# First mixer of a hybrid decoder: where state, query and gate rows are loaded from, and when the head norm and the gate transposes run

## The chip, the cores and the metric

The kernel runs on one core of a Trainium2 chip. A core has five engines with a queue of instructions each: TensorE (PE, matrix products and transposes), VectorE (DVE), ScalarE (ACT), GpSimd (POOL) and SyncE (SP). Each engine takes its own instructions in order and waits on semaphores for the others. Transfers are issued by an engine (here SP and GpSimd) and carried out by 16 DMA engines. The metric is the device time of one execution in microseconds, shown as the median of several runs.

## The reference

One inference step of a two-layer decoder. Layer one is an mLSTM mixer, layer two a forgetting-attention mixer, each followed by a SwiGLU FFN. Two request groups go through the same weights: a prompt of 1024 rows behind 16 meta rows, and 8 decode sequences of 8 rows with a saved state (C, n, m) each. The change lies in the first mixer. Per head and per chunk of rows it computes

```
b      = cumsum(lf)                                   # log-forget gates
m_t    = max(b + m, max_s(b_t - b_s + li_s))
s      = (q k^T) * exp(b_t - b_s + li_s - m_t)        # causal
num    = exp(b + m - m_t) * (q C) + s v
den    = exp(b + m - m_t) * (q n) + sum(s)
h      = num / max(|den|, exp(-m_t))
C_new  = w_c C + sum_s w_g k_s v_s^T ;  n_new = w_c n + sum_s w_g k_s
out    = (rmsnorm(h, mh_g) * sigmoid(og)) @ w_out     # per head norm, output gate
```

All products are in 32-bit floating point; the large ones are made of three products of a high and a low part of each operand.

## The kernel before

All 1104 rows (64 decode rows, 16 meta rows, 1024 prompt rows) are cut into nine slices (`TT`): slice 0 has the 80 decode and meta rows, slices 1 to 8 have 128 prompt rows each. Three slices make one group (`GRP`, `TS`), of 336, 384 and 384 columns.

`phase_a` projects the values (`tm_proj`), then queries and keys (`qk_out`), whose results ScalarE copies out of PSUM (`qk_evict`, L722) and GpSimd's queue writes to the DRAM scratch `qkD` (L723). `rec_prep` computes the gates: the rows `stk` hold the exponents and weights of all heads over time. They are transposed in nine pieces into `tm` (L958, L959), with one PSUM buffer `tps` per piece and two buffers in rotation; small products `wps` (L962, L963) follow. The rows e and w go to the scratch `eD` and `wD`.

`recurrence` then runs slice by slice, with the order of PE, VectorE, ScalarE and GpSimd fixed as written; SP's queue is ordered by the scheduler. In between it calls `f(n)`, which issues n pieces of the remaining projections (`rest_out`: tile `mmA`, weights `wraw` loaded on SP, `whi` cast on ScalarE at L327, `wlo` subtracted on VectorE at L328). One piece is three products. So PE has filler work while the recurrence waits.

For slice i, `chunk_load` fetches `eb` (the gate rows, broadcast), `qk` and `wb` (the decay weights, broadcast): from SP's queue for slice 0 and from GpSimd's for the others. `chunk_decay` makes the exponents of `eb` (L1130, then ScalarE at L1132); `chunk_scores` computes the scores `sps`, multiplies them into `eb` (L1148), transposes the keys (`kps`, L1152) and scales queries in place into `wb` (L1156). `chunk_state` makes the state products `cp` (L1185) and adds them to C (L1189); GpSimd scales C for the next slice (L1192). `chunk_out` makes the outputs `nps` and copies `den` (L1209) and the values (L1215) out.

Slice 0 also has the eight decode states. `first_load` fetches state C (eight transfers, L1110) and n (four, L1112), both on SP's queue. `first_queries` writes the scaled queries `wb` to the scratch `qwD` (L1164, GpSimd) and reads them back in another layout into `q2` (L1168, four transfers on SP). `first_sums` transposes n on PE (`n0p`, L1119). In `chunk_out` VectorE copies parts of q2 into `qm` (L1228), which PE multiplies with the saved states (`nps`, L1233).

After every third slice `norm_heads` normalizes the heads of a group: a few small steps on `fA`, then one multiplication for each of the three slices (L1329). In the loop over slices its steps are taken by `next(norm)` at two places, and at the end of the next slice by a loop that takes all that are left.

From slice 6 on, `g` takes the place of `f`: it issues the filler and one `gate` step. A gate step works on one head of one group: a row of the output gate (`ogc`, from the scratch `ogD`, on GpSimd's queue, L787, four buffers), its sigmoid on ScalarE (L788), a transpose of the head (`ghps`, L1351), the product (L1353) and the split into high and low parts (L340, L341). `ahead()` fetches one row; it is called twice behind slice 5, and then inside `gate` until three rows are ready.

Of the kernel before, what the change touches and what calls it, by code (L numbers as in the profile page):

```python
# [7 lines left out]
F32 = mybir.dt.float32  # L8
# [8 lines left out]
P = 128  # L17
# [659 lines left out]
def phase_a(self, vt):  # L677
# [6 lines left out]
    with ExitStack() as c3:  # L684
# [93 lines left out]
        def heads(pp, tag, op, deep):  # L778
            ready, behind = [], []
            todo = [(t, h) for t in (0, 1, 2) for h in left[t]]  # L780

            def ahead():
                if todo:
                    t, h = todo.pop(0)
                    og = op(self.uid("ogc"))
                    og = og[:, : TS[t][1] - TS[t][0]]
                    nc.gpsimd.dma_start(og, ogD[h, :, TS[t][0] : TS[t][1]])  # L787
                    ready.append([og, lambda: nc.scalar.activation(og, og, AF.Sigmoid)])  # L788
                    if deep == 1:
                        ready[-1].pop()()  # L790

            def rest():
                while behind:
                    behind.pop(0)()

            def gate(t):
                if not left[t]:
                    return False
                while todo and len(ready) < 1 + deep:
                    ahead()  # L800
                for x in ready[: deep]:
                    if len(x) > 1:
                        x.pop()()
                part = self.gate_head(t, left[t].pop(0), v, ready.pop(0)[0], pp, tag)
                if deep > 1:
                    rest()
                behind.append(part)
                if deep == 1:
                    rest()
                return True  # L810
            return gate, ahead, rest
# [39 lines left out]
def rec_prep(self, kp, gates, rp, pp):  # L851
# [3 lines left out]
    if True:  # L855
# [45 lines left out]
        if True:  # L901
# [51 lines left out]
                                    in1=e[:, T0 + P - 1 : T : P].unsqueeze(2).broadcast_to([HA, 8, P]), op=ALU.add)  # L953
            nc.scalar.activation(stk[64:72], b, AF.Exp)
            yield
            for i, (t0, t1) in enumerate(TT):
                ps = pp.tile([P, 104], F32, name=self.uid("tps"), tag="r")
                nc.tensor.transpose(ps[: t1 - t0], stk[:, t0:t1], self.ident[:104, :104])  # L958
                nc.vector.tensor_copy(tm[: t1 - t0, i, :], ps[: t1 - t0])  # L959
            ps = pp.tile([P, 2, 4, 8], F32, name="wps", tag="r")  # L960
            for j in range(4):
                nc.tensor.matmul(ps[:, 0, j, :], selP[:, j, :], w[:, T0 + P - 1 : T : P], start=True, stop=True)  # L962
# [7 lines left out]
def recurrence(self, kp, rec, v, qkD, fill, gate):  # L970
# [7 lines left out]
    def f(n):  # L978
        for _ in range(n):
            next(fill, None)  # L980
        done[0] += n
# [7 lines left out]
    with ExitStack() as cr, self.pool("recAp", bufs=2, space=PSUM) as pp, \  # L989
# [24 lines left out]
        with self.pool("rec2") as sets[2], self.pool("rec1", bufs=2) as rp, self.pool("rec3") as sets[0], \  # L1014
# [9 lines left out]
            for i in range(1, NT):  # L1024
                if i == 4:
                    upto(8 * KT)
                N2 = load(i + 2) if i + 2 < NT else None
                if i + 1 < NT:
                    f(4 if i > 1 else 8)
                    some()  # L1030
                    self.chunk_scores(i + 1, N, rp, *args, f)
                some()
                next(norm, None)
                g(3)
                some()
                self.chunk_state(i, R, *args, wcP, g)
                if i == NT - 1:
                    nn = rp.tile([P, 4], F32, name="nn", bufs=1)
                    nc.vector.tensor_copy(nn, C[i % 2][:, :, DV])
                if N2:  # L1040
                    self.chunk_decay(i + 2, N2, tm, cap)
                next(norm, None)
                for _ in squares:
                    pass
                squares = self.chunk_out(i, R, rp, *args, den, ssq, g, exp=N2 and N2["exp"])
                if i % 3 == 2:
                    for _ in squares:
                        pass
                next(squares, None)
                for _ in norm:  # L1050
                    pass
                norm = self.norm_heads(i // 3, v, rp) if i % 3 == 2 else iter(())
                if i == 5:
                    ahead()
                    ahead()
                    upto(24 * KT)
                    g = lambda n: f(n) or gate(0) or gate(1)
                R, N = N, N2
            rest()
            next(norm)  # L1060
# [19 lines left out]
def chunk_load(self, i, rp, pp, kp, C, v, qkD, eD, wD, tm, eb=None):  # L1080
    nc = self.nc
    t0, t1 = TT[i]
    L = t1 - t0
    q = nc.gpsimd if i else nc.sync
    if eb is None:
        eb = rp.tile([P, HA, P], F32, name=f"eb{i}", tag="eb", bufs=2 if i % 3 == 1 or i == 0 else None)
    qw = rp.tile([P, 4, P], F32, name=f"wb{i}", tag="wb")
    kw = rp.tile([P, HA, DK], F32, name=f"kw{i}", tag="kw")
    qk = rp.tile([P, 8, P], F32, name=f"qk{i}", tag="qk")
    q.dma_start(eb[:L, :, :L], eD[:, t0:t1].partition_broadcast(L))  # L1090
    q.dma_start(qk[:, :, :L], qkD[:, :, t0:t1].rearrange("m p t -> p m t"))
    for a in range(2):
        q.dma_start(qw[a * 64 : a * 64 + 64, :, :L], wD[a::2, t0:t1].partition_broadcast(64))
    return dict(qk=qk, eb=eb, qw=qw, kw=kw)


# [1 line left out]
def first_load(self, R, sp):  # L1098
# [10 lines left out]
        for j in range(4):  # L1109
            nc.sync.dma_start(C0[a * 64 : a * 64 + 64, j, :, :DV], I["state_C"][0, 2 * j + a].rearrange("h k v -> k h v"))  # L1110
    for j in range(4):
        nc.sync.dma_start(n0[j * 8 : j * 8 + 8], I["state_n"][0, 2 * j : 2 * j + 2].rearrange("a h k -> h a k"))  # L1112


@_add(Net)
# [43 lines left out]
@_add(Net)  # L1159
def first_queries(self, R, sp):  # L1160

    nc = self.nc
    qd = self.dram.tile([P, 4, NS], F32, name="qwD")
    nc.gpsimd.dma_start(qd, R["qw"][:, :, :NS])  # L1164
    q2 = R["q2"]
    for a in range(2):
        for z in range(2):
            nc.sync.dma_start(q2[a * 64 : a * 64 + 64, :, z, :], qd[z * 64 : z * 64 + 64])  # L1168
    for qm in R["qms"]:
        nc.gpsimd.memset(qm, 0.0)  # L1170


@_add(Net)
# [1514 lines left out]
```

## Time and profile before

| | us |
|---|---|
| median of 3 runs | 2926.47 |
| lowest and highest run | 2926.18, 2928.61 |
| the profiled execution | 2928.52 |
| span of the profile (first to last instruction) | 2926.8 |
| TensorE busy in the span | 2825.8 |
| VectorE, ScalarE, GpSimd busy | 1721.1, 1312.4, 1006.0 |
| mean granted clock of TensorE | 0.990 |

The gate transposes run near 183 us of the span, slice 0 from about 218 to 294 us, the loop over the slices until about 457 us. In the rows of the trace a line starts with the start and the length in microseconds, then engine, line, operation, output and inputs; `x8` is the number of instructions in the row, and brackets hold the idle time of the engine before it and what ended it. Rows of SPq and POOL with DMA_DIRECT2D are issues of transfers, not the transfers. Rows of a table by stretches hold the busy time of PE, PEld (weight loads), DVE, ACT and POOL, the granted clock, the busy share of the DMA engines and GB/s.

### The profile page before, as it was taken

What the parts mean: (1) busy time and instruction counts of PE and PEld (TensorE: products, weight loads), DVE (VectorE), ACT (ScalarE), POOL (GpSimd) and SP (SyncE); (2) the same over time, 40 slices, a digit from 0 to 9 for tenths busy, and PEclk for the clock granted to TensorE, in tenths of its full rate; (3) what the DMA queues carried; (4) which work ended last, traced back from release to release, by engine and by line L of the source; (5) the groups of instructions that cost most, each with busy time, mean ns of one, the idle gap of its engine ahead of it and who ended that gap; (6) DMA issues with size and microseconds to landing.
All of it is one profiled execution on the core that took longest, in us unless ns stands there. A gap on an engine that the chain in (4) does not pass through costs nothing.

```text
span 2926.8 us, 53724 instructions
## 1 busy us (share of the span) xinstructions
PE 2825.8 (97%) x20542; PEld 2700.4 (92%) x20542; DVE 1721.1 (59%) x3422; ACT 1312.4 (45%) x2620; POOL 1006.0 (34%) x1481
## 2 busy tenths in 40 slices
PE   7998999999999999999999899999999999999998
PEld 7997988999999999999999887777899999999998
DVE  5044555887777755552355443777468778775543
ACT  5122454544444434443344454877344444443432
POOL 2021333165656411115352101454306565641110
PEclk9999999999999999999999999999999999999999
DMA  7047655222222275543443675342412222227652
GB/s 223 9 121 166 168 159 158 79 79 76 88 80 79 86 268 194 204 142 126 144 164 125 225 287 213 129 167 86 147 53 83 77 83 82 77 86 254 218 182 100
DMA packets 316843, 401.37 MB, mean 137 GB/s; under 512 B 32510, under 2 KB 239354, under 8 KB 315562
## 3 DMA queue, kind: packets, MB, share of 16 engines
q1 hardware_dynamic: 279618, 278.44, 29.6%
q0 software_dynamic: 33296, 117.20, 12.1%
q8 instruction: 161, 2.64, 0.4%
q10 hardware_dynamic: 3672, 2.31, 0.3%
q14 instruction: 96, 0.79, 0.1%
HBM read 300.78 MB, written 97.10 MB: 136 GB/s over the span
## 4 chain that ended last, share of the span: by engine, by line
PE 74%; DVE 11%; issue 5%; DMA 5%; ACT 4%; POOL 1%; SPq 0%; DVEq 0%; ACTq 0%; POOLq 0%
PE m L1410 23%; PE dps L267 6%; PE dps L266 6%; PE dps L268 6%; PE tmps L268 4%; PE tmps L266 4%; PE tmps L267 4%; PE mmA L266 2%; PE mmA L267 2%; DVE slot L341 2%; PE mmA L268 2%; PE sp L2475 2%; PE op L2562 1%; DVE s L2479 1%; PE bps L266 1%
## 5 line engine op out<-in xcount | busy, mean ns | idle before, releaser
L341 DVE TENSOR_TENSOR slot<-slot,slot 128x1024 fp32r<-128x1024 f32 (+3 forms) x263 | 268.4, 1023 | 128.5 <-ACT slot L340 122.2
L340 ACT CAST slot<-slot 128x1024 fp32r<-128x1024 f32 (+3 forms) x263 | 206.6, 788 | 230.1 <-PE dps L267 90.3
L1410 PE MATMUL m<-x1h,slot 128*128 128x384 f32 x640 | 177.8, 338 | 1.6 <-DVE vA L1385 0.8
L1410 PE MATMUL m<-x0h,slot 128*128 128x336 f32 x640 | 167.2, 316 | 0.0
L1410 PE MATMUL m<-x2h,slot 128*128 128x384 f32 x480 | 136.0, 338 | 0.0
L413 POOL TENSOR_TENSOR ns<-ns,nq 128x384 f32<-128x384 f32 (+1 forms) x60 | 65.1, 1086 | 206.0 <-ACT nq L411 204.7
L1517 POOL DMA_DIRECT2D hr<-hT x60 | 32.6, 543 | 287.7 <-DVE T_2l L341 70.9
L108 POOL TENSOR_TENSOR slot<-Ht 128x256 f32<-128x256 f32 x80 | 76.9, 971 | 149.2 <-DMA Ht<-in_w_gate_up 144.4
L108 POOL TENSOR_TENSOR slot<-vA 128x256 f32<-128x256 f32 x80 | 75.3, 952 | 149.4 <-DMA vA<-in_w_gate_up 76.5
L341 DVE TENSOR_TENSOR slot<-vA,slot 128x256 fp32r<-128x256 f32 (+3 forms) x101 | 85.3, 846 | 61.9 <-ACT slot L340 61.9
L341 DVE TENSOR_TENSOR slot<-Ht,slot 128x256 fp32r<-128x256 f32 (+3 forms) x101 | 85.3, 846 | 61.7 <-ACT slot L340 61.7
L1410 PEld LDWEIGHTS m<-x1h,slot 128*128 128x128 f32 x640 | 117.3, 188 | 2.8 <-DVE Ht L1385 1.3
L1410 PEld LDWEIGHTS m<-x0h,slot 128*128 128x128 f32 x640 | 113.6, 188 | 0.0
L1410 PE MATMUL m<-x1l,slot 128*128 128x384 f32 x320 | 108.0, 337 | 0.0
L1410 PE MATMUL m<-x0l,slot 128*128 128x336 f32 x320 | 101.5, 317 | 0.0
L1410 PE MATMUL m<-T_2h,slot 128*128 128x384 f32 x320 | 97.0, 344 | 3.8 <-ACT Ht L1416 1.1
L2502 ACT ACTIVATE s<-s,nb 128x272 f32<-128x272 f32 (+7 forms) x126 | 98.9, 787 | 0.0
L2537 ACT COPY th<-tp 128x768 f32<-128x768 f32 (+1 forms) x80 | 73.4, 919 | 53.5 <-PE tp L2529 30.5
L1410 PE MATMUL m<-T_4h,slot 128*128 128x384 f32 x320 | 96.6, 343 | 0.0
L108 POOL TENSOR_TENSOR vA<-vA 128x512 f32<-128x512 f32 (+1 forms) x60 | 85.1, 1419 | 28.4 <-DVE wl0l L341 28.4
L108 POOL TENSOR_TENSOR Ht<-Ht 128x512 f32<-128x512 f32 (+1 forms) x60 | 84.9, 1416 | 28.4 <-DVE wl1l L341 28.4
L1929 DVE TENSOR_REDUCE ss<-sqb 128x4 f32<-128x256 f32 (+1 forms) x72 | 30.2, 419 | 108.2 <-ACT sqb L1928 107.8
(819 smaller groups left out, 10355.2 us busy)
## 6 DMA issues: line engine op xcount, KB each, us to landing
slot<-in_w_down SPq DMA_DIRECT2D x88, 512.0 KB, 4.1
wr<-in_w_down SPq DMA_DIRECT2D x42, 512.0 KB, 5.1
wraw<-in_w_in_a SPq DMA_DIRECT2D x40, 512.0 KB, 3.9
vA<-in_w_gate_up SPq DMA_DIRECT2D x40, 512.0 KB, 4.0
Ht<-in_w_gate_up SPq DMA_DIRECT2D x40, 512.0 KB, 3.9
hr<-hT POOLq DMA_DIRECT2D x46, 384.0 KB, 5.0
kp<-in_cache_k SPq DMA_DIRECT2D x32, 512.0 KB, 6.3
vp<-in_cache_v SPq DMA_DIRECT2D x32, 512.0 KB, 5.6
```

The costliest lines, as they stand in the source:

```text
L108: self.net.nc.gpsimd.tensor_tensor(out=o, in0=a, in1=b, op=op)
L266: mm(ps, sh, mh, start=first, stop=False)
L267: mm(ps, sh, ml, start=False, stop=False)
L268: mm(ps, sl, mh, start=False, stop=last)
L340: self.nc.scalar.copy(hi, src)
L341: self.nc.vector.tensor_tensor(out=lo, in0=src, in1=hi.bitcast(F32), op=ALU.subtract)
L413: (nc.vector if x >= late else nc.gpsimd).tensor_tensor(out=s, in0=s, in1=sq, op=ALU.add)
L1410: nc.tensor.matmul(u.b[b][:, :n], w[p][:, k], x[q][:, k], start=new and k == i == 0, stop=k == 1 and i == 2, skip_group_check=True)
L1517: nc.gpsimd.dma_start(hraw[j], hT[t][:, 2 * c : 2 * c + 2])
L2475: nc.tensor.matmul(ps[z][:, :n], a[r, qs], b[r, at : at + n], start=(y == 0), stop=(y == 2))
L2502: nc.scalar.activation(ss[z, u], ss[z, u], AF.Exp, bias=nb[:, z : z + 1], accum_out=sm[:, u, z : z + 1])
L2537: nc.scalar.copy(th.rearrange("p x z (u h q) -> p h (x z u) q", h=2, q=64)[:, :, :n], pt[:, :, :n])
```

## The change

Four things change, all in the first mixer.

*State and query loads.* For slice 0, `eb` and `wb` are loaded from GpSimd's queue and only `qk` from SP's; the four loads of n and the four loads of q2 move from SP's queue to GpSimd's, the latter behind the two fills of `qm`.

Before, on SP, between the weight loads `wraw` of the filler:

```order
L324 DMA wraw_2659<-in_w_in_a 128x8x128
L1090 DMA eb_2585<-eD 80x8x80
L1091 DMA qk_2588<-qkD 128x8x80
L1093 DMA wb_2586<-wD 64x4x80 x2
L1110 DMA C_2602<-in_state_C 64x8x128 x8
L1112 DMA n_2603<-in_state_n 8x2x64 x4
L1168 DMA q_2594<-qwD 64x4x64 x4
L324 DMA wraw_2720<-in_w_in_a 128x8x128
```

After, on SP:

```order
L324 DMA wraw_2647<-in_w_in_a 128x8x128
L1096 DMA qk_2576<-qkD 128x8x80
L1113 DMA C_2590<-in_state_C 64x8x128 x8
L324 DMA wraw_2708<-in_w_in_a 128x8x128
L324 DMA wraw_2765<-in_w_in_a 128x8x128
```

SP goes from the state C straight to the weights. On GpSimd, after the change, between the writes of `qkD` (before, the same stretch held only those writes, the write of `qwD` and the two fills):

```order
L723 DMA qkD<-stg_2509 128x336
L1090 DMA eb_2573<-eD 80x8x80
L723 DMA qkD<-stg_2537 128x384
L1094 DMA wb_2574<-wD 64x4x80 x2
L1115 DMA n_2591<-in_state_n 8x2x64 x4
L723 DMA qkD<-stg_2644 128x384
L1167 DMA qwD<-wb_2574 512x1x64
L1170 MEMSET qm_2583 128x400
L1170 MEMSET qm_2584 128x400
L1173 DMA q_2582<-qwD 64x4x64 x4
L723 DMA qkD<-stg_2705 128x384
L1195 TENSOR_TENSOR C_2561<-C_2559,wcP 128x516
```

The eleven moved issues stand ahead of the scaling of C, and q2 stands ahead of one more write of `qkD`.

*Gate rows.* `ahead()` now fetches until three rows are ready (two where `heads` is used in the FFN's first part), is called once behind slice 5, and then at the start of every `g`, ahead of the filler. On GpSimd before, at the loads of slice 8:

```order
L787 DMA ogc_4169<-ogD 128x336
L787 DMA ogc_4171<-ogD 128x336
L749 DMA ogD<-stg_4185 128x384
L1090 DMA eb_4188<-eD 128x8x128
L1091 DMA qk_4191<-qkD 128x8x128
L1093 DMA wb_4189<-wD 64x4x128 x2
L749 DMA ogD<-stg_4253 128x384
L787 DMA ogc_4265<-ogD 128x336
L1192 TENSOR_TENSOR C_2573<-C_2571,wcP 128x516
```

and after:

```order
L787 DMA ogc_4157<-ogD 128x336
L787 DMA ogc_4159<-ogD 128x336
L787 DMA ogc_4161<-ogD 128x336
L749 DMA ogD<-stg_4175 128x384
L1090 DMA eb_4178<-eD 128x8x128
L1094 DMA qk_4181<-qkD 128x8x128
L1094 DMA wb_4179<-wD 64x4x128 x2
L749 DMA ogD<-stg_4243 128x384
L1195 TENSOR_TENSOR C_2561<-C_2559,wcP 128x516
```

The third row goes ahead of two writes of `ogD` and four loads.

*Norm.* The loop that took all remaining steps of `norm_heads` takes one. So in the slice after a group only the first multiplication is done at its end, and the second and third come in the next slice: behind the scaled queries (L1156) and behind `chunk_decay`. This holds for the first two groups.

*Gate transposes.* The nine pieces share three PSUM buffers (slice 0, slices 1 to 4, slices 5 to 8), with one copy by VectorE for each. The diff:

```diff
             def ahead():
-                if todo:
+                while todo and len(ready) < 1 + deep:
                     t, h = todo.pop(0)
                     og = op(self.uid("ogc"))
                     og = og[:, : TS[t][1] - TS[t][0]]
                     nc.gpsimd.dma_start(og, ogD[h, :, TS[t][0] : TS[t][1]])
-                    ready.append([og, lambda: nc.scalar.activation(og, og, AF.Sigmoid)])
+                    ready.append([og, lambda og=og: nc.scalar.activation(og, og, AF.Sigmoid)])
...
-                while todo and len(ready) < 1 + deep:
-                    ahead()
+                ahead()
...
-            for i, (t0, t1) in enumerate(TT):
-                ps = pp.tile([P, 104], F32, name=self.uid("tps"), tag="r")
-                nc.tensor.transpose(ps[: t1 - t0], stk[:, t0:t1], self.ident[:104, :104])
-                nc.vector.tensor_copy(tm[: t1 - t0, i, :], ps[: t1 - t0])
+            for i0, i1 in ((0, 1), (1, 5), (5, NT)):
+                ps = pp.tile([P, 4, 104], F32, name=self.uid("tps"), tag="r")
+                L = TT[i0][1] - TT[i0][0]
+                for i in range(i0, i1):
+                    nc.tensor.transpose(ps[:L, i - i0, :], stk[:, TT[i][0] : TT[i][1]], self.ident[:104, :104])
+                nc.vector.tensor_copy(tm[:L, i0:i1, :], ps[:L, : i1 - i0])
...
-                for _ in norm:
-                    pass
-                norm = self.norm_heads(i // 3, v, rp) if i % 3 == 2 else iter(())
+                next(norm, None)
+                if i % 3 == 2:
+                    norm = self.norm_heads(i // 3, v, rp)
                 if i == 5:
                     ahead()
-                    ahead()
                     upto(24 * KT)
-                    g = lambda n: f(n) or gate(0) or gate(1)
+                    g = lambda n: ahead() or f(n) or gate(0) or gate(1)
...
-    q = nc.gpsimd if i else nc.sync
+    q = nc.gpsimd
...
-    q.dma_start(qk[:, :, :L], qkD[:, :, t0:t1].rearrange("m p t -> p m t"))
-    for a in range(2):
-        q.dma_start(qw[a * 64 : a * 64 + 64, :, :L], wD[a::2, t0:t1].partition_broadcast(64))
+    loads = [(qk[:, :, :L], qkD[:, :, t0:t1].rearrange("m p t -> p m t"))]
+    loads += [(qw[a * 64 : a * 64 + 64, :, :L], wD[a::2, t0:t1].partition_broadcast(64)) for a in range(2)]
+    for o, src in loads if i else loads[1:]:
+        q.dma_start(o, src)
+    if i == 0:
+        nc.sync.dma_start(*loads[0])
...
-        nc.sync.dma_start(n0[j * 8 : j * 8 + 8], I["state_n"][0, 2 * j : 2 * j + 2].rearrange("a h k -> h a k"))
+        nc.gpsimd.dma_start(n0[j * 8 : j * 8 + 8], I["state_n"][0, 2 * j : 2 * j + 2].rearrange("a h k -> h a k"))
...
+    for qm in R["qms"]:
+        nc.gpsimd.memset(qm, 0.0)
     for a in range(2):
         for z in range(2):
-            nc.sync.dma_start(q2[a * 64 : a * 64 + 64, :, z, :], qd[z * 64 : z * 64 + 64])
-    for qm in R["qms"]:
-        nc.gpsimd.memset(qm, 0.0)
+            nc.gpsimd.dma_start(q2[a * 64 : a * 64 + 64, :, z, :], qd[z * 64 : z * 64 + 64])
```

## The prediction

> **What bounds the kernel now.** I read the page first, then the busy time by stretches, then the waits of TensorE inside the first mixer, then the rows around each wait.
>
> ```profile
> span 2926.8 us, 53724 instructions
> ...
> PE 2825.8 (97%) x20542; PEld 2700.4 (92%) x20542; DVE 1721.1 (59%) x3422; ACT 1312.4 (45%) x2620; POOL 1006.0 (34%) x1481
> ```
>
> ```profile
> 150.00:480.00 330.00, 306.71 (x2041) 281.31 (x2040) 169.01 (x380) 133.43 (x334) 86.66 (x135) 0.96 0.60 160
> 480.00:2926.80 2446.80, 2386.26 (x17448) 2289.31 (x17447) 1509.87 (x2982) 1124.40 (x2171) 902.19 (x1289) 0.99 0.40 135
> ```
>
> TensorE (PE) is the bound: busy 97% of the span. The change touches only the stretch 150 to 480 us (columns: length, then busy time of PE, weight loads, VectorE, ScalarE, GpSimd; then the granted clock). There PE is idle for 330.0 - 306.7 = 23.3 us, and its clock is 0.96, worth another 330 x 0.04 = 13 us. So at most 36 us, 1.2% of the span, lie in this stretch. What is won there should reach the end, because behind it PE is busy 97.5% of the time (2386.3 of 2446.8).
>
> ```profile
> PE n0p L1119 <- DMA n<-in_state_n: 6.2, 1, 6.2
> PE kps L1152 <- DVE eb L1148: 3.1, 2, 2.4
> PE mmA L266 <- ACT stg L748: 2.9, 2, 2.4
> ...
> PE tps L958 <- DVE tmA L959: 0.8, 4, 0.3
> ```
>
> These are the waits of PE in that stretch that the change aims at (total, times, longest): one of 6.2 us for the state vector n, two for VectorE before the scores, one of 2.4 us for ScalarE's eviction, four short ones in the gate transposes. Together 13 us.
>
> ```profile
> 182.00:186.00 4.00, 3.17 (x18) 2.22 (x17) 1.77 (x9) 0.75 (x2) 0.54 (x1) 1.00 1.01 309
> 186.00:194.00 8.00, 8.00 (x31) 7.81 (x32) 1.67 (x4) 0.75 (x1) 0.00 (x0) 0.57 0.28 79
> ...
> 236.00:246.00 10.00, 9.23 (x44) 8.83 (x45) 1.89 (x3) 2.75 (x5) 1.07 (x1) 0.57 0.52 131
> ...
> 404.00:410.00 6.00, 4.77 (x26) 4.43 (x27) 2.58 (x7) 2.97 (x7) 1.75 (x4) 0.72 0.58 178
> ...
> 418.00:422.00 4.00, 3.84 (x16) 3.63 (x16) 2.00 (x4) 1.66 (x10) 0.00 (x0) 0.58 0.47 135
> ...
> 458.00:462.00 4.00, 2.09 (x12) 1.82 (x13) 1.23 (x1) 2.06 (x3) 1.09 (x2) 1.00 0.64 208
> ```
>
> Behind the waits stands a second loss: the granted clock (third number from the end) falls. The price of each dip is its length times the missing clock: 8 x 0.43 = 3.4 us at 186, 10 x 0.43 = 4.3 at 236, 6 x 0.28 = 1.7 at 404, 4 x 0.42 = 1.7 at 418. Each follows a thin stretch of PE. But the last row shows a stretch in which PE was busy 2.09 of 4 us and kept clock 1.00, so a dip isn't certain behind a gap of that size.
>
> [...]
>
> **Gate transposes.** Nine copies become three, and PE no longer stops for a free bank after every second transpose: 0.8 us of waits go. The matrix product behind them (wps) now needs the bank of the middle group, a copy four times as long as before; below one of the old waits, 0.3 us. I take 0.6 (bounds 0.3 to 0.8). The thin stretch that ends in the dip at 186 gets shorter by that but keeps its small products, so of the 3.4 us I book half, 1.7 (bounds 0 to 3.4).
>
> **State and query loads.** Here is today's order: two pieces of the chain that ended last (the second is one product of PE at full clock), then rows of PE, SP's queue, GpSimd, ScalarE and VectorE, each with start and length:
>
> ```profile
> 229.68 6.85 DMA n<-in_state_n
> ```
>
> ```profile
> 199.44 0.17 PE mmA L266
> ```
>
> ```profile
> 236.77 0.28 PE L1119 MATMUL n0p<-ident,n 32*128 32x32 f32 x1 [6.20 <-DMA n<-in_state_n]
> 236.98 1.98 PE L1185 MATMUL cp<-vA,kw 16*64 16x129 f32 x16
> ...
> 246.81 1.08 PE L1233 MATMUL nps<-C,qm 128*80 128x129 f32 x8
> ```
>
> ```profile
> 220.14 7.13 SPq L1110 DMA_DIRECT2D C<-in_state_C  x8
> 227.32 3.81 SPq L1112 DMA_DIRECT2D n<-in_state_n  x4
> 236.34 2.51 SPq L1168 DMA_DIRECT2D q<-qwD  x4
> 238.95 34.03 SPq L324 DMA_DIRECT2D wraw<-in_w_in_a  x7
> ```
>
> ```profile
> 229.38 0.74 POOL L1164 DMA_DIRECT2D qwD<-wb  x1 [4.49 <-DVE wb L1156]
> ```
>
> ```profile
> 243.25 1.04 ACT L327 CAST whi<-wraw 128x1024 fp32r<-128x1024 f32 x1 [13.67 <-DMA wraw<-in_w_in_a]
> ```
>
> ```profile
> 244.33 1.22 DVE L328 TENSOR_TENSOR wlo<-wraw,whi 128x1024 fp32r<-128x1024 f32 x1 [7.02 <-ACT whi L327]
> 245.47 1.24 DVE L1228 COPY qm<-q 64x32 f32<-64x32 f32 x2
> ```
>
> n is issued behind eight state loads on the same queue and lands at 236.5. On GpSimd's queue it is issued before 225, ahead of the wait for wb, so PE does not stop at n0p. But the next need is the query copy q2: qwD is written at 229.4, SP waits for it until 236.3, and that wait is only hidden by the wait for n. Without it PE goes on from 230.5: n0p and cp (1.4 us at full clock), 24 products at 0.17 us (4.1), and it stands before nps at about 236.9. So what is late next is q2. It can't be issued before 236.3 (nothing makes qwD earlier), and four issues last 2.5 us as on SP, since GpSimd issues such transfers in 0.54 to 0.74 us.
>
> ```profile
> DMA to landing us min/median/max: 2.3/2.3/2.3
> ```
>
> ```profile
> DMA to landing us min/median/max: 3.8/7.1/7.6
> ```
>
> ```profile
> DMA to landing us min/median/max: 10.2/10.2/10.2
> ```
>
> From issue to landing these are q (from SP, its queue empty), wb (lowest from SP, the others from GpSimd beside big loads) and C. Bounds for q2 from GpSimd are 2.3 and 7.6 us; one weight load will still be under way on SP's queue, which is free of q2's wait now and so issues the weights at about 226 instead of 239. I take 3.5: landing at 238.2 + 3.5 = 241.7, qm copied by 242.2, nps at 242.5. VectorE's other step ahead of qm, wlo, gives the same time: weights issued behind C, whose last load lands at about 225 + 10.2 = 235, then 4.3 us for the weights as now (238.95 to 243.25), 1.0 and 1.2 us for the two casts: 241.7. So nps starts 4.3 us earlier than 246.8, and PE waits some 5.6 us at a new place. A clock dip will follow it. Today's dip is over before nps; the new one falls on work behind it. Price between the small dips (1.7) and today's (4.3): 3.0. Net 4.3 - 3.0 = 1.3 us, bounds -4.1 (q2 at 7.6: 4.1 us later, so nps at 246.6 and a full dip) and 10.5 (no wait and no dip: 6.2 + 4.3).
>
> The other moved issues: eb, wb and n of the first slice go between the evictions on GpSimd, by their order in the new program. eb, issued behind the eviction at about 216.5,
>
> ```profile
> L1130 DVE SCALAR_TENSOR_TENSOR eb<-eb,tmA,cap x8: 288/290/296, 205.8 to 207.3; 80x80 f32<-80x80 f32 x8
> ```
>
> ```profile
> 225.35 0.88 DVE L1148 TENSOR_TENSOR eb<-sps,eb 80x320 f32<-80x320 f32 x2 [16.66 <-PE sps L1146]
> ```
>
> at wb's highest price of 7.6 lands at 224; its eight decays (0.29 each, 2.3) and an exponent of no more than a cast's 1.0 would end at 227.4, and VectorE's product with the scores, which starts at 225.4 today, would be 2.0 us late; at the lowest, 3.8, it lands at 220.3 and nothing is late. I take nothing, and 2.0 is in the range. GpSimd stands at q2 until 236.3; queued behind it are one eviction, whose buffer is needed three tiles on, and the first state product, which waits for ScalarE until 244.9 today. Both cost nothing unless q2 is issued after that.
>
> **Gate rows.** The third gate row was issued behind an eviction; now it goes with the first two, twelve microseconds earlier.
>
> ```profile
> 395.24 0.55 POOL L787 DMA_DIRECT2D ogc<-ogD  x1
> ...
> 399.54 0.58 POOL L787 DMA_DIRECT2D ogc<-ogD  x1
> ```
>
> ```profile
> 401.92 0.48 ACT L788 ACTIVATE ogc<-ogc 128x336 f32<-128x336 f32 x1 [1.48 <-DMA ogc<-ogD]
> ...
> 404.69 0.49 ACT L748 COPY stg<-mmA 128x384 f32<-128x384 f32 x1
> ```
>
> ScalarE waited 1.48 us for that row; three table loads around it stay. The eviction at 404.7, for which PE waits 2.4 us, comes at most 1.5 us earlier; the fourth row, issued at 399.5, needs about as long and lands just in time, so I take 0.9 (bounds 0 to 1.5). With the gap at 1.5 us I let the dip at 404 go: 1.7 (bounds 0, 1.7). The later rows move past one eviction at a time, but wait for a buffer that is freed no earlier; nothing.
>
> **Norm dealt out.** The same six multiplications; two of each three move to later places on VectorE.
>
> ```profile
> 352.04 3.50 DVE L1329 TENSOR_TENSOR vA<-vA,fA 80x1024 f32<-80x1024 f32 x3
> ...
> 412.88 3.50 DVE L1329 TENSOR_TENSOR vA<-vA,fA 128x1024 f32<-128x1024 f32 x3
> ...
> 417.43 1.28 DVE L1148 TENSOR_TENSOR eb<-sps,eb 128x512 f32<-128x512 f32 x2
> ```
>
> ```profile
> 414.69 1.04 ACT L327 CAST whi<-wraw 128x1024 fp32r<-128x1024 f32 x1
> ```
>
> Each block shrinks from 3.5 to 1.2 us. At 357 PE waited 0.7 us (3.1 - 2.4), all of it goes. At 418 VectorE's next step is wlo, and that needs ScalarE's cast, which ends at 415.7; so it can begin only 0.6 us earlier than now. I take 0.7 + 0.6 = 1.3 (bounds 0.7 and 3.1). The dip at 418 stays. The moved pieces stand ahead of state sums and den copies where VectorE idles 1 to 2 us before them; nothing.
>
> **Sum.** 0.6 + 1.3 + 0.9 + 1.3 = 4.1 us of waits, and 1.7 + 1.7 = 3.4 of clock: 7.5. The profiled execution took 2928.5 us (span 2926.8, 1.7 around it), at the upper end of the three runs (2926.2 to 2928.6, median 2926.5). From the median: 2919.0 us.
>
> **Rivals.**
> - The clock is not won (for: a gap of 1.9 us at 458 without dip, so dips follow something else than wait length; against: each dip here stands behind a thin stretch): 2926.5 - 4.1 = 2922.4. [...]
> - The wait for n turns whole into a wait for q2, nps no earlier (for: qwD's 6.9 us is untouched). The term 1.3 becomes -3.0: 7.5 - 4.3 = 3.2, 2923.3.
> - Slower: GpSimd's transfers get little of the engines while C and two weight loads stand on SP's queue, each taking C's 10.2 us: wb, issued at 222, lands at 232, qwD at 243.5, q2 (issued until 245.4) at 255.6, and nps starts at 256.2, 9.4 us later than now, with today's dip of 4.3 behind it. 1.3 becomes -13.7, the sum 7.5 - 15.0 = -7.5: 2934.0. It is a loss from q2 landing at about 248, and one over the bound below from about 254. Against: wb took 7.1 us beside such loads, qwD 6.9 beside C. [...]
> - Better: q2 comes early and no dip follows, all the waits go: 0.6 + 3.4 + 10.5 + 0.9 + 1.7 + 1.3 = 18.4, 2908.1.
>
> **Chances.** A measurement of this kernel tells a change from none at about 0.2%, 5.9 us: faster is below 2920.6, slower above 2932.3. Forecast 0.41, clock not won 0.24, whole wait for q2 0.14, slower 0.11, better 0.10. Faster is the forecast, the better case and a fourth of the second: 0.57; slower is the fourth, 0.11; the rest, 0.32, is within. The range goes from near the better case to the upper side of the q2 case with eb's 2.0 us late: 2909 to 2927.
>
> **What would show it.** PE's wait at n0p is gone and stands at nps for qm, near 242, for 4 to 7 us, the clock half behind it; no wait at tps; the wait for the eviction near 400 under 1.7 us with clock 1.00; the wait before kps near 415 shorter by half a microsecond. Wrong would be: PE still stopping at n0p (wb's and n's landing), a stop at kps near 227 (eb late), or the stretch behind 480 longer than 2446.8.

## The result and the profile after

The changed kernel takes 2912.7 us (median of 5 runs, 2908.4 to 2914.3). The kernel before, run beside it on the same chip, takes 2926.5 us (5 runs, 2924.7 to 2928.6). The ratio is 0.9951, with a 95% interval of 0.9937 to 0.9966: 13.7 us faster. The forecast was 2919.0, 7.5 us faster. The profiled execution of the changed kernel took 2914.3 us, 1.6 above the median.

The page of the changed kernel, its first lines:

```profile
span 2912.4 us, 53731 instructions
...
PE 2819.3 (97%) x20542; PEld 2696.0 (93%) x20542; DVE 1717.8 (59%) x3416; ACT 1312.6 (45%) x2620; POOL 1009.4 (35%) x1492
```

Busy time by stretches, changed kernel (columns as before: length, PE, PEld, DVE, ACT, POOL, granted clock, DMA share, GB/s):

```profile
150.00:480.00 330.00, 314.43 (x2130) 291.48 (x2131) 175.50 (x385) 136.45 (x342) 99.33 (x155) 0.98 0.63 167
480.00:2912.40 2432.40, 2370.90 (x17353) 2273.66 (x17351) 1499.61 (x2970) 1119.74 (x2162) 892.97 (x1280) 0.99 0.41 135
```

In the stretch of the change PE now idles 15.6 us instead of 23.3, and the clock is 0.98 instead of 0.96. The waits of PE there, changed kernel (total, times, longest):

```profile
PE nps L1236 <- POOL C L1195: 3.3, 1, 3.3
PE mmA L266 <- ACT stg L748: 3.2, 2, 2.0
PE n0p L1122 <- DMA n<-in_state_n: 1.6, 1, 1.6
...
PE wps L963 <- DVE tmA L960: 0.2, 1, 0.2
```

The 6.2 us at n0p have become 1.6 there and 3.3 at nps. The stops at tps and at kps are gone. One of the two stops for ScalarE's eviction has shrunk to 1.25 us; the other, of 2.0 us, is new in size (0.6 before). Now the granted clock (third number from the end) at the places of the old dips, and of a new one at 422:

```profile
186.00:190.00 4.00, 4.00 (x16) 4.00 (x15) 0.83 (x1) 0.00 (x0) 0.00 (x0) 0.57 0.46 130
190.00:194.00 4.00, 4.00 (x27) 4.00 (x26) 0.87 (x1) 2.33 (x3) 0.54 (x1) 1.00 0.13 45
...
236.00:242.00 6.00, 4.67 (x24) 4.63 (x25) 1.64 (x7) 1.15 (x2) 4.64 (x6) 0.72 0.93 216
...
396.00:402.00 6.00, 6.00 (x46) 5.44 (x44) 3.16 (x9) 4.21 (x9) 1.39 (x3) 1.00 0.61 178
402.00:406.00 4.00, 3.92 (x34) 3.48 (x34) 3.85 (x6) 3.98 (x12) 1.07 (x2) 1.00 0.37 90
...
422.00:426.00 4.00, 4.00 (x27) 3.35 (x26) 1.09 (x2) 3.10 (x9) 0.54 (x1) 0.60 0.63 181
```

The dip at 186 lasts 4 us instead of 8; the one at 236 costs 6 x 0.28 = 1.7 us instead of 4.3; those at 404 and 418 are gone; the one at 422 (4 x 0.40 = 1.6 us) stands behind the stop of 2.0 us.

That stop is the old one of 404 at a later place: in ScalarE's order the eviction stands behind the sigmoid of a gate row, and the sigmoid waited 2.41 us for the row. ScalarE, changed kernel:

```profile
418.03 0.53 ACT L788 ACTIVATE ogc<-ogc 128x384 f32<-128x384 f32 x1 [2.41 <-DMA ogc<-ogD]
...
420.09 0.50 ACT L748 COPY stg<-mmA 128x384 f32<-128x384 f32 x1
```

To see where the 13.7 us lie, I take the start of the same PE instruction in both traces. The column of differences grows where time is won. 1.6 us are there before anything that the change touches, and belong to no stage.

| same instruction of PE | start before | start after | difference | won in this stage |
|---|---|---|---|---|
| csps, ahead of the change | 150.06 | 148.46 | 1.60 | |
| first wps, behind the gate transposes | 185.89 | 182.81 | 3.08 | 1.5 |
| first sps of slice 0 | 224.44 | 219.99 | 4.45 | 1.4 |
| n0p | 236.77 | 227.72 | 9.05 | |
| first nps with qm | 246.81 | 237.34 | 9.47 | 5.0 |
| first nps of the third head | 251.58 | 243.63 | 7.95 | -1.5 |
| kps of slice 4 | 357.33 | 348.50 | 8.83 | 0.9 |
| ghps near 411 | 410.94 | 399.49 | 11.45 | 2.6 |
| kps near 418 | 418.16 | 404.44 | 13.72 | 2.3 |
| cp behind it | 422.18 | 406.89 | 15.29 | 1.6 |
| last row of the mixer compared | 498.95 | 483.55 | 15.40 | 0.1 |

From 1.60 to 15.40 are 13.8 us, about as much as the medians differ (13.7). From the last row to the end of the span both kernels take about the same (2427.9 and 2428.8 us).

### The profile page after: what moved, and what is told of

Read it like the earlier page. It is cut to its first block, busy times and chain, and to the rows that moved or that the text cites. A ratio compares the mean times of both kernels' runs of the same rounds, so it can differ in the third digit from the quotient of the medians.

```text
span 2912.4 us, 53731 instructions
## 1 busy us (share of the span) xinstructions
PE 2819.3 (97%) x20542; PEld 2696.0 (93%) x20542; DVE 1717.8 (59%) x3416; ACT 1312.6 (45%) x2620; POOL 1009.4 (35%) x1492
## 4 chain that ended last, share of the span: by engine, by line
PE 74%; DVE 11%; DMA 5%; issue 5%; ACT 4%; POOL 1%; ACTq 0%; DVEq 0%; POOLq 0%; SPq 0%
PE m L1413 23%; PE dps L267 6%; PE dps L266 6%; PE dps L268 6%; PE tmps L266 4%; PE tmps L268 4%; PE tmps L267 4%; PE mmA L266 2%; DVE slot L341 2%; PE mmA L267 2%; PE mmA L268 2%; PE sp L2478 1%; PE op L2565 1%; DVE s L2482 1%; PE bps L266 1%
```

## The experiments

In the expectations, A is the reading of the table above (each part wins what its stage shows) and B the rival that the text names. Each profiled execution was compared with the one of the kernel before in the same way. Stages, in us won:

| kernel | transposes 150-224 | loads 224-252 | norm, 252-357 | gate rows 357-411 | norm, 411-422 | 422-499 |
|---|---|---|---|---|---|---|
| changed | 2.9 | 3.5 | 0.9 | 2.6 | 3.8 | 0.1 |
| after_again | 2.8 | 3.5 | 0.7 | 2.6 | 3.3 | 1.1 |
| only_tps | 2.9 | -0.2 | -0.3 | 1.9 | 0.0 | 0.0 |
| only_loads | 0.1 | 4.9 | -0.1 | 0.0 | 1.6 | -0.7 |
| only_gate | -0.1 | 0.2 | 0.0 | 2.6 | 0.1 | 0.5 |
| only_norm | 1.4 | 0.3 | 0.9 | 0.4 | 3.8 | -1.5 |
| no_norm | 1.4 | 3.6 | -0.3 | 2.6 | -0.6 | 1.6 |
| no_tps | 1.4 | 5.1 | 0.7 | 2.6 | 3.8 | 0.3 |
| q2_sp | 1.4 | -2.3 | 0.5 | 2.6 | 3.8 | -2.7 |
| c_first | -12.2 | 7.2 | 0.7 | 2.6 | 3.8 | -1.1 |
| direct_q2 | 2.9 | 2.2 | 0.9 | 2.6 | 3.6 | 0.7 |

Each row is one execution: that of only_loads took 2915.3 us where its kernel's median is 2922.2, that of q2_sp 2926.9 where the median is 2920.9. Two cells show a gain in a kernel that lacks the part for that stage: 1.9 in only_tps (357-411) and 1.6 in only_loads (411-422). There PE stopped (1.98 us at 401.8 and 2.35 us at 410.9), but the clock stayed at 1.00 behind the stop. PE and the stretch behind it, only_loads:

```profile
410.88 0.66 PE L1155 MATMUL kps<-ident,qk 128*128 128x128 f32 x4 [2.35 <-DVE eb L1151]
```

```profile
411.00:415.00 4.00, 4.00 (x36) 3.62 (x37) 3.28 (x8) 1.39 (x9) 0.00 (x0) 1.00 0.50 135
```

So a dip can also stay away by itself. Of the four kernels without the gate rows three have the dip behind that eviction, and of the five without the norm's part four have the one behind kps; the eight with the gate rows and the seven with the norm's part have none there.

**Each part alone.** Four kernels, each the one before with one part of the change.

only_loads:

```diff
-    q = nc.gpsimd if i else nc.sync
+    q = nc.gpsimd
...
+    for o, src in loads if i else loads[1:]:
+        q.dma_start(o, src)
+    if i == 0:
+        nc.sync.dma_start(*loads[0])
...
-        nc.sync.dma_start(n0[j * 8 : j * 8 + 8], I["state_n"][0, 2 * j : 2 * j + 2].rearrange("a h k -> h a k"))
+        nc.gpsimd.dma_start(n0[j * 8 : j * 8 + 8], I["state_n"][0, 2 * j : 2 * j + 2].rearrange("a h k -> h a k"))
...
-            nc.sync.dma_start(q2[a * 64 : a * 64 + 64, :, z, :], qd[z * 64 : z * 64 + 64])
...
+            nc.gpsimd.dma_start(q2[a * 64 : a * 64 + 64, :, z, :], qd[z * 64 : z * 64 + 64])
...
```

> Only the state and query loads are moved. Theory A (each part works by itself, and the offsets between the two traces tell its worth): 3.5 us faster than before, 2923.0; TensorE stops less than 2 us at n0p and 3 to 4 us at nps for the query copy, the clock dip behind it costs under 2 us. Theory B (the loads only bring the wait from one place to another, the offset was won by what the transposes shifted ahead): within 1.5 us of before, nps starts no more than 2 us earlier.

only_gate:

```diff
-                if todo:
+                while todo and len(ready) < 1 + deep:
...
-                while todo and len(ready) < 1 + deep:
-                    ahead()
+                ahead()
...
-                    ahead()
                     upto(24 * KT)
-                    g = lambda n: f(n) or gate(0) or gate(1)
+                    g = lambda n: ahead() or f(n) or gate(0) or gate(1)
```

> Only the gate rows are fetched ahead. Theory A: 2.6 us faster than before, 2923.9; the wait for the eviction near 404 falls from 2.4 to about 1.3 us and the clock stays at 1.00 there; the wait of 2.4 us at kps behind it stays. Theory B (the waits from 400 to 420 hang together: a shorter first wait also shortens the one at kps): 4 us or more.

only_norm:

```diff
-                for _ in norm:
-                    pass
-                norm = self.norm_heads(i // 3, v, rp) if i % 3 == 2 else iter(())
+                next(norm, None)
+                if i % 3 == 2:
+                    norm = self.norm_heads(i // 3, v, rp)
```

> Only the norm is dealt out. Theory A: the wait at kps near 418 goes whole, since the weights' low part on VectorE needs a cast that is long done: 2.3 us and its clock dip 1.6, and 0.9 at 357: 4.8 us faster, 2921.7. Theory B (the prediction's: VectorE's low part waits for ScalarE's cast of that moment, and only with the gate rows ahead does the wait go): 1.3 us, and TensorE still stops about 1.8 us at kps.

only_tps:

```diff
-            for i, (t0, t1) in enumerate(TT):
-                ps = pp.tile([P, 104], F32, name=self.uid("tps"), tag="r")
...
+            for i0, i1 in ((0, 1), (1, 5), (5, NT)):
+                ps = pp.tile([P, 4, 104], F32, name=self.uid("tps"), tag="r")
...
```

> Only the gate transposes are put in three groups. Theory A: 2.9 us faster, 2923.6; the products behind the transposes run 1.5 us earlier, and the stretch of half clock is one of about 3.4 us instead of two. Theory B (the length of the dip has nothing to do with the waits and differs from run to run): 0.6 to 1.5 us, and a dip of 7 us as before.

Against 2926.0 us (33 runs) they took, in 11 runs each: only_loads 2922.2, ratio 0.9988 [0.9979, 0.9997]; only_gate 2923.0, 0.9988 [0.9979, 0.9997]; only_norm 2922.7, 0.9988 [0.9979, 0.9997]; only_tps 2926.7, 1.0001 [0.9992, 1.001]. So three parts win 3 to 4 us each, and the transposes nothing that this measurement shows. The four medians add up to 9.4 us, 4.3 less than the whole; the intervals, 2.6 us to either side for each part, don't exclude 13.7. The times alone don't tell A from B here; the rows do, for three of the parts.

In only_loads nps comes 5.1 us earlier in its stage, which excludes B; PE stops there for 1.6 us, not for 3 to 4. In only_tps neither reading fits whole: wps comes 1.5 us earlier and the dip is short, as A says, and yet no time is won. only_gate, waits of PE between 398 and 404: the stop for the eviction is 1.3 us, as in the changed kernel, where it was 2.4 before. The stop of 2.35 us at kps stays (414.5), so B is out.

```profile
PE mmA L266 <- ACT stg L748: 1.3, 1, 1.3
```

only_norm, PE's kps near 412 without any wait, and the clock behind it:

```profile
412.49 0.66 PE L1152 MATMUL kps<-ident,qk 128*128 128x128 f32 x4
```

```profile
414.00:418.00 4.00, 4.00 (x37) 3.59 (x36) 4.00 (x7) 2.29 (x12) 0.68 (x1) 1.00 0.45 131
```

The norm's part alone removes the stop of 2.4 us there, and with the stop the dip is gone, together 3.8 us. A's mechanism holds; its 4.8 us don't show in the median, which is 3.3 lower.

**The whole without one part.** no_norm is the changed kernel with the old loop over `norm`:

```diff
-                next(norm, None)
-                if i % 3 == 2:
-                    norm = self.norm_heads(i // 3, v, rp)
+                for _ in norm:
+                    pass
+                norm = self.norm_heads(i // 3, v, rp) if i % 3 == 2 else iter(())
```

> The changed kernel without the norm dealt out: three multiplications in one block again. Theory A: 4.8 us slower than the changed kernel (the waits at 357 and at kps come back, with the clock dip behind kps), 2917.5. Theory B (the prediction's size): 1.3 us slower, 2914.0.

no_norm took 2918.0 us (10 runs), ratio 0.9972 [0.9963, 0.9982]: 9.4 us faster than the kernel before, where the whole is 12.6 (after_again, below) to 13.7 faster. That is 3.2 to 4.3 us for the norm, nearer to A than to B; but the intervals overlap, and it is the rows that show the part. PE's kps near 409 stops again and the clock falls behind it:

```profile
409.09 1.11 PE L1155 MATMUL kps<-ident,qk 128*128 128x128 f32 x4 [2.88 <-DVE eb L1151]
```

```profile
410.00:414.00 4.00, 4.00 (x29) 3.77 (x28) 2.06 (x4) 0.99 (x8) 0.00 (x0) 0.68 0.43 124
```

Behind these stages, from 422 to 499, only_norm shows -1.5 and no_norm 1.6 against 0.1: the norm may give back about 1.5 us of its 4.7 there. That column runs from -2.7 to 1.6, so this is not shown.

no_tps is the changed kernel with the old nine pieces, and after_again the changed kernel itself, beside it on the same chip:

```diff
-            for i0, i1 in ((0, 1), (1, 5), (5, NT)):
-                ps = pp.tile([P, 4, 104], F32, name=self.uid("tps"), tag="r")
...
+            for i, (t0, t1) in enumerate(TT):
+                ps = pp.tile([P, 104], F32, name=self.uid("tps"), tag="r")
...
```

> The changed kernel with the nine gate transposes as before. Theory A (the transposes are worth 2.9 us, as the offsets of the traces say, and the part alone only missed it by the scatter of the later stages): 2 to 3.5 us slower than the changed kernel of this call, and a dip of 7 us at 185 again. Theory B (the part alone told it: nothing): within 1 us.

> The changed kernel once more, beside the two others of this call, for a closer value than its first five runs: 13.7 us faster than before if those were typical; 9 to 11 us if the sum of the four parts alone (3.9 + 3.0 + 3.3 - 0.7 = 9.5) is its worth.

no_tps took 2917.6 us (6 runs), ratio 0.9969 [0.9957, 0.9982]; after_again 2914.4 (5 runs, 2908.9 to 2917.8), ratio 0.9959 [0.9946, 0.9973]. By these medians the transposes are worth 3.2 us, by only_tps less than nothing. The traces settle what is regular in it. In all seven kernels with three groups wps comes 1.5 us earlier, in none of the others. The dip behind it is another matter. The stretch 184 to 194 of no_tps (old pieces) and of no_norm (new groups):

```profile
184.00:194.00 10.00, 9.63 (x46) 8.95 (x47) 2.67 (x9) 1.04 (x1) 0.24 (x1) 0.83 0.44 129
```

```profile
184.00:194.00 10.00, 10.00 (x43) 9.95 (x44) 1.59 (x4) 1.63 (x3) 0.54 (x1) 0.67 0.21 60
```

A long dip leaves 0.66 or 0.67 (3.3 to 3.4 us lost), a short one 0.83 (1.7 lost). Short: four of the seven with the new groups, two of the five with the old pieces. So the 1.4 us of clock that the changed kernel won there aren't shown to come from the change. What the part is worth in time stays open, since the intervals of these runs overlap; 1.5 us are regular in the traces.

**Who holds q2.** In the changed kernel, PE reaches nps near 234 and stands until 237.3. Rows of PE, GpSimd, SP's queue, ScalarE and VectorE, changed kernel:

```profile
227.72 0.22 PE L1122 MATMUL n0p<-ident,n 32*128 32x32 f32 x1 [1.60 <-DMA n<-in_state_n]
...
237.34 1.87 PE L1236 MATMUL nps<-C,qm 128*80 128x129 f32 x8 [3.26 <-POOL C L1195]
```

```profile
224.93 0.75 POOL L1167 DMA_DIRECT2D qwD<-wb  x1 [4.36 <-DVE wb L1159]
...
232.80 2.47 POOL L1173 DMA_DIRECT2D q<-qwD  x4 [6.31 <-DMA qwD<-wb]
...
235.84 1.15 POOL L1195 TENSOR_TENSOR C<-C,wcP 128x516 f32<-128x516 f32 x1
```

```profile
214.94 9.07 SPq L1113 DMA_DIRECT2D C<-in_state_C  x8
```

```profile
233.78 1.05 ACT L327 CAST whi<-wraw 128x1024 fp32r<-128x1024 f32 x1 [8.65 <-DMA wraw<-in_w_in_a]
```

```profile
234.86 1.22 DVE L328 TENSOR_TENSOR wlo<-wraw,whi 128x1024 fp32r<-128x1024 f32 x1 [6.66 <-ACT whi L327]
236.48 0.76 DVE L1231 COPY qm<-q 64x32 f32<-64x32 f32 x2 [0.40 <-DMA q<-qwD]
```

The view names the scaling of C as the releaser, but VectorE's copy of q2 into qm ends later (237.2 against 237.0). That copy waited only 0.4 us for q2, because VectorE was at wlo until 236.1: q2 and the weights arrive almost together. From the write of qwD to the first issue of q2 pass 7.9 us.

q2_sp puts the four loads of q2 back on SP's queue; the rest is the changed kernel.

```diff
-            nc.gpsimd.dma_start(q2[a * 64 : a * 64 + 64, :, z, :], qd[z * 64 : z * 64 + 64])
+            nc.sync.dma_start(q2[a * 64 : a * 64 + 64, :, z, :], qd[z * 64 : z * 64 + 64])
```

> The changed kernel, but the four query copies q2 stay on SP's queue, ahead of the weights. Theory A (the queue of q2 counts because the weights stand behind it: the weights are issued at 235, their cast and low part end at about 241.5, and the query copies on VectorE stand behind those): nps starts about 4 to 5 us later than in the changed kernel, and it is 3 to 5 us slower, 2916.5. Theory B (only the landing of the scratch qwD counts, whichever queue reads it back): within 1 us of the changed kernel, 2912.7.

It took 2920.9 us (11 runs) against 2927.4 (26 runs), ratio 0.9981 [0.9972, 0.999]. Waits of PE and rows of SP's queue and ScalarE, q2_sp:

```profile
PE nps L1236 <- POOL C L1195: 7.9, 1, 7.9
```

```profile
233.72 2.50 SPq L1173 DMA_DIRECT2D q<-qwD  x4
236.32 20.45 SPq L324 DMA_DIRECT2D wraw<-in_w_in_a  x5
```

```profile
240.62 1.04 ACT L327 CAST whi<-wraw 128x1024 fp32r<-128x1024 f32 x1 [13.40 <-DMA wraw<-in_w_in_a]
```

SP stands at q2 until 233.7, and the cast of the weights behind it comes 6.8 us later than in the changed kernel (2.1 of which this execution was behind already at the scores). In the trace that turns a gain of 3.5 us in this stage into a loss of 2.3. VectorE's wlo, and the copy into qm behind it, wait for that cast. So A holds. q2_sp is 6.4 us faster than the kernel before, where the whole is 12.6 to 13.7; by these medians the price is 6 to 7 us, and the intervals leave A's 3 to 5 open. What the move of q2 does is to let the weights go; with n, eb and wb moved alone this trace wins nothing. Whether the move of q2 would win anything without that of n was not run.

c_first asks why qwD takes 7.9 us. State C is put ahead of all other loads in the program, to have landed before qwD is written:

```diff
+            R0 = {}
+            self.first_load(R0, sp)
             R = self.chunk_load(0, r0, *args)
...
-            self.first_load(R, sp)
+            R.update(R0)
+            for j in range(4):
+                nc.gpsimd.dma_start(R["n0"][j * 8 : j * 8 + 8], I["state_n"][0, 2 * j : 2 * j + 2].rearrange("a h k -> h a k"))
...
```

> The changed kernel, but the eight loads of the state C are issued on SP ahead of the first slice's qk, so that they don't run beside wb, n and qwD. Theory A (qwD takes 7.8 us because the state's 2 MB stand in the DMA engines): C is issued at about 200 and lands by 213, n lands before TensorE needs it, qwD lands in 4 us or less, q2 by 233, and TensorE does not stop at n0p and at most 1 us at nps: 1.6 + 3.3 us of waits and 1.7 of clock go, 6 us faster than the changed kernel, 2906.5. Theory B (qwD's time is that of 512 small pieces on GpSimd's queue, beside whatever): qwD takes 6 us or more, nps waits as now, only the 1.6 us at n0p go: 2911.

It took 2924.1 us (11 runs), ratio 0.999 [0.9981, 0.9999]. C could not go earlier, since its place is in use until PE is done with what stood there, and qk stood behind it. Waits of SP's queue, then rows of PE and GpSimd, c_first:

```profile
SPq L1117 <- PE mmA L268: 18.8, 1, 18.8
```

```profile
235.66 1.36 PE L1151 MATMUL sps<-qk 64*80 64x80 f32 x16 [13.53 <-DMA qk<-qkD]
```

```profile
242.34 0.75 POOL L1169 DMA_DIRECT2D qwD<-wb  x1 [19.80 <-DVE wb L1161]
...
245.02 2.47 POOL L1175 DMA_DIRECT2D q<-qwD  x4 [1.12 <-DMA qwD<-wb]
```

As a version it fails, but it answers the question: written when C has landed, qwD takes 2.7 us instead of 7.9, against B. C's eight loads, issued there from 217.0 to 226.5, take 8.9 to 10.9 us to land, so they are in by about 237, five us ahead of the write. In the changed kernel they are issued until 224.0 and take 10.3 to 10.5 us, and the DMA share from 225 to 233 is 1.18. So in these two traces its time goes with the load of C beside it.

direct_q2 tries to win what is left: q2 is read straight from `qkD`, without qwD, its decay weights come from `wD` as a second tile (in the place of `km`), and VectorE multiplies the two; the first copy into qm stands ahead of the filler.

```diff
+            nc.gpsimd.dma_start(R["q2"][a * 64 : a * 64 + 64, :, z, :],
+                                qkD[:4, z * 64 : z * 64 + 64, :NS].rearrange("m p t -> p m t"))
+    nc.gpsimd.dma_start(R["w2"].rearrange("p j z t -> p (j z) t"), wD[:, :NS].partition_broadcast(P))
...
+    nc.vector.tensor_tensor(out=R["q2"], in0=R["q2"], in1=R["w2"], op=ALU.mult)
...
```

> The changed kernel, but q2 is read from the scratch of the queries itself with its decay weights beside it, and multiplied on VectorE, so that the scaled queries no longer go out to DRAM and back; the first query copy stands ahead of the weights' low part on VectorE. Theory A (the round trip of qwD is what TensorE waits for at nps): the 3.3 us at nps and its clock dip of 1.7 go, 5 us faster than the changed kernel of this call. Theory B (the state C itself lands no earlier: 224 + 10.4 = 234.4, and VectorE's multiplication waits for five more loads on GpSimd's queue): TensorE stops at nps or n0p for as long as before, within 1.5 us.

It took 2916.1 us (5 runs), ratio 0.9964 [0.9951, 0.9978], against 2914.4 for the changed kernel beside it: no gain. Rows of GpSimd and VectorE, direct_q2:

```profile
227.36 0.93 POOL L1122 DMA_DIRECT2D km<-wD  x1 [2.41 <-PE mmA L268]
```

```profile
235.66 0.69 DVE L1175 TENSOR_TENSOR q<-q,km 128x512 f32<-128x512 f32 x1 [10.78 <-DMA km<-wD]
```

The weights tile is issued when its place is free and lands 8.3 us later, beside C again: another load in place of the old wait. That is B's case: PE's stops at n0p and nps add up to 4.5 us, against 4.9 in the changed kernel. No version that I ran beats the changed kernel.

## Why the prediction was right, and where its sizes were off

The direction, the range and the main mechanism held; the gain was 13.7 us instead of 7.5. By stages no term came out smaller than booked, so the total doesn't rest on errors that cancel: 3.2 us more came from the norm at 418, 2.2 from the loads, 0.6 from the transposes and 0.2 from the norm at 357. By its own steps:

- **Gate rows: right.** 0.9 of wait and 1.7 of clock were booked, 2.6; the stage shows 2.6 (1.1 of it wait), and only_gate alone 2.6. The clock's share is less certain than booked, since in only_tps the dip stayed away without the part. And the later rows, booked at nothing, are the next limit: now that the stops ahead are gone, one of them holds ScalarE for 2.41 us at 418 and PE for 2.0 behind it. The signs named came: the eviction's wait is 1.25 us (under 1.7) and the clock 1.00 from 396 to 406.

Changed kernel, the third row's issue on GpSimd, its sigmoid and the eviction on ScalarE, and PE behind it:

```profile
374.56 1.61 POOL L787 DMA_DIRECT2D ogc<-ogD  x3
```

```profile
391.56 0.48 ACT L788 ACTIVATE ogc<-ogc 128x336 f32<-128x336 f32 x1
...
394.70 0.49 ACT L748 COPY stg<-mmA 128x384 f32<-128x384 f32 x1
```

```profile
395.25 0.44 PE L266 MATMUL mmA<-x2h,whi 128*128 128x384 f32 x1 [1.25 <-ACT stg L748]
```

- **Norm at 418: wrong, the largest miss** (0.6 booked, 3.8 measured; only_norm and no_norm both show it). The step that failed is "VectorE's next step is wlo, and that needs ScalarE's cast, which ends at 415.7; so it can begin only 0.6 us earlier". Changed kernel, VectorE, then ScalarE:

```profile
401.43 1.22 DVE L1332 TENSOR_TENSOR vA<-vA,fA 128x1024 f32<-128x1024 f32 x1
402.57 1.22 DVE L328 TENSOR_TENSOR wlo<-wraw,whi 128x1024 fp32r<-128x1024 f32 x1
403.70 1.28 DVE L1151 TENSOR_TENSOR eb<-sps,eb 128x512 f32<-128x512 f32 x2
```

```profile
395.07 1.07 ACT L327 CAST whi<-wraw 128x1024 fp32r<-128x1024 f32 x1
...
403.48 1.03 ACT L327 CAST whi<-wraw 128x1024 fp32r<-128x1024 f32 x1
```

wlo starts at 402.57, before the cast at 403.48 begins, so it belongs to the cast that ended at 396.1. I had paired it with the cast that stands next to it in time; its own had been done for 10 us in the kernel before as well. There wlo starts at 416.29, and its cast is this one:

```profile
405.06 1.06 ACT L327 CAST whi<-wraw 128x1024 fp32r<-128x1024 f32 x1
```

wlo was held by VectorE's own order alone, the whole 2.3 us went, and with the stop went the dip of 1.7 that I let stay (in only_loads a dip stayed away there without the part, in the four others it came). The upper bound given, 3.1 for both places, left the dip out too.

- **Norm at 357: right.** 0.7 booked; 0.9 measured in the changed kernel and in only_norm.

- **State and query loads: mechanism right, size too small.** Net 1.3 booked, 3.5 measured (4.9 in only_loads, 5.1 in no_tps). As said, the wait for n became a wait for q2, half the clock stands behind it, eb came in time, and the weights went ahead on SP. qwD took 7.9 us, a microsecond more than assumed, but the four loads of q2 landed in 2.4 to 3.6 us and everything was there 3.7 us after the first issue, where I had 5.4; so nps came 5.0 us earlier in its stage, not 4.3. The working's stretch from n0p to the stop at nps, 6.4 us, came as said, though the terms listed for it add up to 5.5. The larger share is the new dip: 1.5 us, not the 3.0 taken between 1.7 and 4.3. In only_loads the dip fell on the filler ahead of nps (clock 0.83 from 226 to 236, 1.00 from 236 to 242), inside time that PE would have waited anyway (stops of 1.6 and 1.6 us), and cost nothing. One sign of "wrong" did come, and "so PE does not stop at n0p" was false: PE stops there for 1.6 us, since n, issued from 217.6 on, takes 8 us to land. It should cost nothing, because the wait at nps, set by q2 and the weights, is shorter by it; no run tests that.

- **Gate transposes: half right.** 0.6 of waits and 1.7 of clock were booked, 2.9 measured in the changed kernel. The waits gave what was booked: 0.84 went and 0.2 came, at wps, as named. But the nine transposes also run through:

```profile
181.43 1.18 PE L959 MATMUL tps<-ident,stk 104*80 104x104 f32 x9
182.81 0.35 PE L963 MATMUL wps<-wA,selP 8*128 8x8 f32 x2 [0.20 <-DVE tmA L960]
```

In the kernel before they are five short rows of 0.34, 0.48, 0.48, 0.48 and 0.31 us, 2.1 together:

```profile
183.01 0.34 PE L958 MATMUL tps<-ident,stk 104*80 104x104 f32 x2
183.62 0.48 PE L958 MATMUL tps<-ident,stk 104*128 104x104 f32 x2 [0.27 <-DVE tmA L959]
...
185.63 0.31 PE L958 MATMUL tps<-ident,stk 104*128 104x104 f32 x1 [0.19 <-DVE tmA L959]
```

Now they are one row of 1.2. That is another 0.9 us which the view of waits doesn't hold. The clock's share came in this execution, but the twelve traces don't show that it came from the change; that this term fits is luck.

- **The rivals.** "The wait for n turns whole into a wait for q2" is excluded by nps, 5.0 us earlier. "Slower" needed q2 to land at 248 or later; it landed before 236.5. The loads on GpSimd's queue were not starved: beside C, issued on SP's queue from 214.9 to 224.0 and 10.3 to 10.5 us on its way, n landed in 7.7 to 8.4 us, and q2, issued from 232.8 on, in 2.4 to 3.6. "The clock is not won" is excluded by the clock of 1.00 at the places of the old dips at 404 and 418. What remains of it: a new stop of 2.0 us at 420.6 is followed by a dip, 1.6 us that were not on the list, and the stretch from 422 to 499 gave no more than 0.1. The stretch behind the mixer took 2428.8 us against 2427.9, inside its scatter over the twelve traces. "Better" is nearest in time (2908.1 against 2912.7, the forecast is 6.3 off), but not what happened: PE still waits 3.3 us at nps, with a dip behind it.

## What to carry to other kernels

Before a wait is called the next limit, follow the tile and not the neighbour in time: an operand in rotating buffers may have been ready one round earlier, and only the start of the instruction in another order shows it. When a load is taken off a queue, look first at what it was holding up behind it: here the move of n won nothing in a trace as long as the weights stood behind q2. Here 20 of 35 stops of PE of 1.3 to 2.9 us (twelve traces, 394 to 460 us) had a dip behind them that cost another 1.7 us in clock, so price a wait with its dip, but expect a single dip to be there in one execution and not in the next. And when two stops are gone, look for the one that the same engine order makes a little later: here ScalarE's wait for the next gate row.

## What the runs showed of the hardware

In these traces dips of the clock come in units. From 184 to 194 the loss was 1.7 us in six executions (clock 0.83) and 3.3 to 3.4 in six others (0.66 or 0.67), once or twice the same amount. Around the waits of slice 0 it was 1.8 us in the changed kernel (222 to 252), an estimated 3.3 in direct_q2 (from the starts of its products, 0.32 us apart instead of 0.17: 1.6 from 230.8 to 234.2 and 1.7 from 240.6 to 244.5), and 5.1 to 5.2 in the kernel before, only_gate and only_norm, which load n on SP's queue (226 to 246). Between 394 and 460 us the twelve traces have 20 dips of 1.7 us each. Thirteen stand behind single stops of PE of 1.8 to 2.9 us, and seven behind stops of 1.3 to 1.6; five and ten stops of these sizes had no dip behind them, nor had the eight of about 1.25 us for the eviction near 400. One of the seven is at 446 in the kernel before, and the changed kernel has one at the same time.

The same kernel scatters by about 4 us to either side. The 59 runs of the kernel before beside the first seven experiments lay between 2922.8 and 2931.7 us. In the twelve traces the part behind the mixer, where the instructions are the same, took 2422.3 to 2431.3 us. So a change of 3 us takes tens of runs, or the comparison of starts above, to be seen.

A write of the queries to DRAM and its completion took 2.7 us when the state had landed (c_first) and 7.9 beside its load (changed kernel); the dependent loads issued from GpSimd landed in 2.4 to 3.6 us in the changed kernel and 3.8 to 4.5 in c_first, against 2.3 from SP in the kernel before.
